# The entry of a streaming encoder trunk: memory keys and values in one loop, smaller first tiles, another inverse root

## The chip, the cores and the metric

One Trainium2 chip; the program runs on one of its cores. The metric is the device time of one execution in microseconds (us). A core has five engines with instruction queues of their own, each worked off in order: TensorE (PE in the profile, its weight loads PEld), VectorE (DVE), ScalarE (ACT), GpSimd (POOL) and SyncE (SP). They meet only at semaphores. Copies between the main memory and the core's two on-chip memories are issued here by SP, POOL and, in a few places, ACT. TensorE reads from the larger on-chip memory and writes its sums to eight banks of the smaller one, the PSUM.

## What is computed

The reference is a two-layer encoder for 512 tokens of width 1024, in float32. Only its beginning matters here:

```
def reference(x, mem, norm_mix_g, norm_ffn_g, a_w_in, ..., mem_w_kv, ...):
    for l in range(DEPTH):
        h = rmsnorm(x, norm_mix_g[l])
        if l < N_A_LAYERS:
            proj = h @ a_w_in[a]
            ...
        mem_out = memory_attention(q_mem, mem, mem_w_kv[l])
...
def memory_attention(q, mem, w_kv):
    mk, mv = jnp.split(mem @ w_kv, 2, axis=-1)
```

`mem` is 256 by 1024, `mem_w_kv` two matrices of 1024 by 512 (256 columns of keys, 256 of values). Since `mem @ mem_w_kv[l]` needs nothing of `x`, the kernel does it for both layers at its very start, while `x` is still being loaded. `rmsnorm` divides each row of `x` by the root of its mean square, so it needs one inverse root for each of the 512 tokens.

## The kernel before, in words

**Three products for one.** Every float32 matrix product is done as three products of shorter numbers. `split` (lines 139 to 144) makes of a tile its rounded high part, by a copy on ACT (line 140), and the rest, its low part, by a subtraction on DVE (line 141). `mm3` (lines 192 to 196) then issues high by high, high by low and low by high, one after the other, into the same PSUM bank. So a tile from memory can be used a first time when ACT has made its high part, a second time when DVE has made a low part, and so on.

**The entry** is lines 355 to 375 (loads) and 447 to 517. The loads are issued by SP in the order of the program: for q from 0 to 3 a tile `memr[q]` of the memory rows (256 KB) and a tile `kraw[q]` of the first layer's key weights (256 KB), then four tiles `vraw` of its value weights (256 KB each), two tiles `kraw1` of the second layer's key weights (512 KB each), `x` in four tiles of 512 KB, two tiles `vraw1` of the second layer's value weights, and from there the weights of the first projection. The three buffers tagged `wr` hold the 512 KB tiles in turn.

From line 447 on, the order of PE, ACT and DVE is that of the program: nothing is moved within each of these engines. It is:

- six small products of ones (`warm`, line 453), then a loop over q (lines 457 to 474): four transposes of `memr[q]` into one bank (line 462), `split` of the transposed tile, `split` of `kraw[q]`, and then the twelve key products of tile q - 1. In the first turn three more products of ones stand in their place. So the products of one tile hide the splitting of the next.
- a loop over the four value tiles (lines 476 to 481): `split`, then twelve value products each; between them, DVE copies the finished keys out of their two banks (`keep`, line 395), and POOL writes them to memory.
- `split` of the two `kraw1` tiles into the weight buffers `wh`/`wl`, and 48 key products of the second layer.
- the squares of `x` by ACT and DVE (lines 408 and 410), their sum and the inverse root `rsqrt` (lines 238 to 247: a shifted integer as a first guess and three steps of Newton, eleven instructions of DVE with 4 columns each), two diagonal matrices of it (line 256), `split` of `vraw1[0]`.
- eight `x_tile`s: four transposes of `x` on PE (line 417), a copy of 512 columns out of the bank by ACT (line 419). The banks go round: even tiles use tag `sc` (3 banks), odd tiles tag `tr` (2 banks), and a 106-column transpose of the small vectors takes a `tr` bank after tile 0. So tile 7 gets the bank that tile 3 had.
- `spread` (line 269): two products that lay the inverse roots along the columns; then the 48 value products of the second layer, from `vws1`, and beside them DVE and ACT scale and split the transposed `x` (lines 427, 432 and 435) for the first projection, `value_columns(1)`, whose first product with `x` is the first instruction of line 194 with 392 columns.

**Everything behind line 517** is ordered by a scheduler, which puts instructions of the later parts where it expects them to be ready. It starts from where the entry leaves the engines, so a change of the entry can move instructions far behind it.

## Time and profile before

| | |
|---|---|
| time, median of 3 runs | 1179.44 us (1178.71 to 1181.65) |
| the profiled execution | 1178.89 us, of which 1177.2 us from the first to the last instruction |
| PE busy | 1167.7 us (99% of the span), 7007 instructions |
| DVE busy | 941.1 us (80%), 1685 instructions |
| ACT busy | 730.3 us (62%), 1295 instructions |
| granted TensorE clock, mean | 0.999 |
| the chain that ended last | PE 95%, DVE 3%, ACT 1% |

The profile lists instructions with the time from the span's start, their duration, engine and line, what they write and read, and in brackets how long the engine had stood idle before and what ended that. Matmuls are pipelined: one of 256 columns lasts 0.28 us, but the next starts 0.12 us later, so the distance between starts says how fast PE goes.

### The profile page before, as it was taken

To read this page: it belongs to the slowest core of one execution; us is meant where nothing else is said; L and a number is where in the kernel's file an instruction comes from. 1 tells how busy PE (TensorE), PEld (TensorE's weight loads), DVE (VectorE), ACT (ScalarE), POOL (GpSimd) and SP (SyncE) were. 2 spreads that over 40 slices of the span, in tenths; PEclk is the share of its full clock that TensorE was granted. 3 is DMA by queue.
4 is the path that set the end of the run, shared out by engine and by line. 5 is a ranking of instruction groups with operands and counts; after the bars stand their busy time and mean duration, and the time that the engine had idled before them with its cause. 6 is when DMAs were issued, how large, how long until landed. Compare 5 with 4: busy or idle time off the path is not lost.

```text
span 1177.2 us, 18659 instructions
## 1 busy us (share of the span) xinstructions
PE 1167.7 (99%) x7007; PEld 1033.4 (88%) x7007; DVE 941.1 (80%) x1685; ACT 730.3 (62%) x1295; POOL 129.6 (11%) x222
## 2 busy tenths in 40 slices
PE   9999999999999999999999999999999999999997
PEld 9988888888889999999888888888889999999986
DVE  6877688887979887777698888897897887777755
ACT  6548677654656656665666667776565665666545
POOL 1111101000021111111020000101001011110100
PEclk9999999999999999999999999999999999999999
DMA  8645325243267766665564312335426456566551
GB/s 301 206 108 136 94 55 152 76 140 120 90 157 153 190 165 162 163 144 128 149 200 126 90 54 85 105 100 179 142 90 153 108 140 140 143 144 144 126 161 72
DMA packets 200445, 158.64 MB, mean 135 GB/s; under 512 B 8377, under 2 KB 180383, under 8 KB 200355
## 3 DMA queue, kind: packets, MB, share of 16 engines
q1 hardware_dynamic: 184194, 119.87, 34.5%
q0 software_dynamic: 15584, 36.67, 15.8%
q8 instruction: 55, 0.90, 0.3%
q10 hardware_dynamic: 576, 0.92, 0.2%
q14 instruction: 36, 0.29, 0.1%
HBM read 128.89 MB, written 32.46 MB: 137 GB/s over the span
## 4 chain that ended last, share of the span: by engine, by line
PE 95%; DVE 3%; ACT 1%; issue 0%; POOL 0%; POOLq 0%; DVEq 0%; ACTq 0%
PE pmm L194 18%; PE pmm L195 18%; PE pmm L196 18%; PE ptr L195 6%; PE ptr L194 6%; PE ptr L196 6%; PE psc L196 5%; PE psc L195 5%; PE psc L194 5%; PE psc L544 2%; PE ptr L1365 1%; PE ptr L1386 1%; PE ptr L1387 1%; PE ptr L627 1%; PE ptr L613 0%; DVE pt L141 0%
## 5 line engine op out<-in xcount | busy, mean ns | idle before, releaser
L194 PE MATMUL pmm<-u,wh 128*128 128x512 f32 (+1 forms) x968 | 333.0, 344 | 0.2 <-ACT u L140 0.2
L196 PE MATMUL pmm<-u,wl 128*128 128x512 f32 (+1 forms) x968 | 330.8, 342 | 0.0
L195 PE MATMUL pmm<-u,wh 128*128 128x512 f32 (+1 forms) x968 | 330.5, 342 | 0.0
L141 DVE TENSOR_TENSOR wl<-wr,wh 128x1024 fp32r<-128x1024 f32 (+3 forms) x172 | 199.8, 1163 | 82.0 <-ACT wh L140 81.5
L140 ACT CAST wh<-wr 128x1024 fp32r<-128x1024 f32 (+3 forms) x172 | 171.9, 1001 | 93.1 <-PE pmm L195 39.6
L196 PEld LDWEIGHTS pmm<-u,wl 128*128 128x128 f32 x968 | 181.9, 188 | 20.8
L194 PEld LDWEIGHTS pmm<-u,wh 128*128 128x128 f32 x968 | 181.8, 188 | 18.7 <-ACT u L140 1.1
L195 PEld LDWEIGHTS pmm<-u,wh 128*128 128x128 f32 x968 | 182.0, 188 | 18.4 <-DVE u L141 0.5
L194 PE MATMUL ptr<-u,wh 128*128 128x512 f32 x272 | 106.4, 391 | 0.0
L195 PE MATMUL ptr<-u,wh 128*128 128x512 f32 x272 | 106.2, 390 | 0.0
L196 PE MATMUL ptr<-u,wl 128*128 128x512 f32 x272 | 105.8, 389 | 0.0
L778 POOL DMA_DIRECT2D xspill<-t x64 | 55.5, 867 | 432.1 <-ACT t L777 419.6
L834 ACT COPY t<-pmm 128x256 f32<-128x256 f32 x102 | 38.2, 374 | 76.7 <-PE pmm L196 76.5
L141 DVE TENSOR_TENSOR u<-t,u 128x512 fp32r<-128x512 f32 (+1 forms) x94 | 54.2, 600 | 35.4 <-ACT u L140 35.4
L194 PE MATMUL pmm<-u,fh 128*128 128x256 f32 x272 | 75.4, 277 | 0.0
L195 PE MATMUL pmm<-u,fh 128*128 128x256 f32 x272 | 75.2, 277 | 0.0
L196 PE MATMUL pmm<-u,fl 128*128 128x256 f32 x272 | 75.1, 276 | 0.0
L196 PE MATMUL psc<-u,wl 128*128 128x256 f32 (+1 forms) x232 | 75.1, 324 | 0.0
L195 PE MATMUL psc<-u,wh 128*128 128x256 f32 (+1 forms) x232 | 75.1, 324 | 0.0
L194 PE MATMUL psc<-u,wh 128*128 128x256 f32 (+1 forms) x232 | 74.9, 324 | 0.0
L141 DVE TENSOR_TENSOR fl<-pt,fh 128x512 fp32r<-128x512 f32 x102 | 70.4, 690 | 5.1 <-ACT fh L140 1.4
L140 ACT CAST fh<-pt 128x512 fp32r<-128x512 f32 x102 | 62.8, 616 | 9.2 <-DVE pt L888 6.0
(334 smaller groups left out, 2509.1 us busy)
## 6 DMA issues: line engine op xcount, KB each, us to landing
wr<-in_ffn_w_up_dram SPq DMA_DIRECT2D x54, 512.0 KB, 6.0
wr<-in_ffn_w_down_dram SPq DMA_DIRECT2D x38, 512.0 KB, 5.5
pt<-in_ffn_w_up_dram SPq DMA_DIRECT2D x34, 512.0 KB, 7.7
xspill<-t POOLq DMA_DIRECT2D x64, 256.0 KB, 4.3
wr<-in_a_w_in_dram SPq DMA_DIRECT2D x20, 512.0 KB, 3.8
wr<-in_w_kv_dram SPq DMA_DIRECT2D x12, 512.0 KB, 4.1
xspill<-fh POOLq DMA_DIRECT2D x16, 256.0 KB, 2.6
xspill<-fl POOLq DMA_DIRECT2D x16, 256.0 KB, 3.1
```

The source lines that it names most:

```text
L140: high = A.copy(hi, src) if on_act else V.tensor_copy(hi, src)
L141: low = V.tensor_tensor(out=lo, in0=src, in1=f(hi), op=ALU.subtract)
L194: nc.tensor.matmul(o, lh, rh, start=first, stop=False, skip_group_check=more)
L195: nc.tensor.matmul(o, lh, rl, start=False, stop=False, skip_group_check=more)
L196: nc.tensor.matmul(o, ll, rh, start=False, stop=last, skip_group_check=more)
L544: nc.tensor.matmul(o, a, b, start=first and i == 0, stop=i == 1)
L627: nc.tensor.matmul(o2, vs[a][:, 2 * hp + h, :], p[h][:, a, :], start=i == 0, stop=i == 3)
L778: G.dma_start(xspill[j], t, accum_op=ALU.add)
L834: A.copy(o, r[:, :H])
L1365: nc.tensor.transpose(tp[:, b * P : (b + 1) * P], es[T, h][:, b * P : (b + 1) * P], ident)
L1386: nc.tensor.matmul(o2[:, s * P :], w, hi_at(pts[h], s, s, TT - s), start=s == 0, stop=False)
L1387: nc.tensor.matmul(o2[:, s * P :], w, lo_at(pts[h], s, s, TT - s), start=False, stop=s == TT - 1)
```

## The change

It is made in the entry alone; all the rest of the program text is as it was.

- **Loads.** The first memory tile and the first key tile come in two halves of 128 KB (one row tile of 128 rows each); one of the four halves is issued by ACT instead of SP. Each value tile is issued right after the key tile of the same q, where before all value tiles came after all key tiles.
- **First step.** Five products of ones instead of six at the start, one instead of three later. The two row tiles of tile 0 are transposed into two banks, and split in pieces of 256 columns. DVE makes the first high part of the keys. The first six products are ordered by part.
- **One loop.** For q from 1 to 3: transposes of tile q, `split` of the transposed tile, of the key tile and of the value tile; then the value products of tile q - 1 and the key products of tile q itself. After the loop: `keep` of the keys, and the last twelve value products.
- **Second keys.** The two `kraw1` tiles are split into the same two weight buffers as before, with the 16 columns of spare room at the end of the high part and at the start of the low part, and not the other way round.
- **Inverse root.** ACT takes the logarithm and the exponential with factor -0.5 (two instructions of 4 columns), DVE makes one Newton step (three instructions). The table of ACT that holds both functions is loaded once, at the start.
- **`vraw1[0]`** is split after the third `x_tile` and no longer ahead of the first, and the second layer's value products are issued in the order of their parts: all high by high, then all low by high, then all high by low.

```diff
         def scale(self, o):
-            v = small()
+            v, r, t, self.col = small(), small(), small(), small()
             V.tensor_scalar(v, o, 1.0 / D, EPS, op0=ALU.mult, op1=ALU.add)
-            self.col = small()
-            rsqrt(self.col, v)
+            A.activation(t, o, AF.Ln, scale=1.0 / D, bias=eps)
+            A.activation(r, t, AF.Exp, scale=-0.5)
+            V.tensor_mul(t, r, r)
+            V.scalar_tensor_tensor(t, t, -0.5, v, op0=ALU.mult, op1=ALU.mult)
+            V.scalar_tensor_tensor(self.col, t, 1.5, r, op0=ALU.add, op1=ALU.mult)
...
+    for i, queue in enumerate((nc.scalar, nc.sync)):
+        load_memory(0, i * P, P)
+        queue.dma_start(kraw[0][:, i : i + 1, :], rows(mem_w_kv[0], 0, MEM, i, i + 1))
+    nc.sync.dma_start(vraw[0], rows(mem_w_kv[0], MEM, MEM, 0, 2))
+    for q in range(1, KT // 2):
+        load_memory(q, 0, MEM)
+        nc.sync.dma_start(kraw[q], rows(mem_w_kv[0], 0, MEM, 2 * q, 2 * q + 2))
+        nc.sync.dma_start(vraw[q], rows(mem_w_kv[0], MEM, MEM, 2 * q, 2 * q + 2))
...
+    def value_products_by_parts(os_, wh, wl, k0):
+
+        n = wh.shape[1]
+        for part, w in ((0, wh), (1, wh), (0, wl)):
+            for k in range(n):
+                for m, o in enumerate(os_):
+                    a = memT[k0 + k][part][:, m * P : (m + 1) * P]
+                    first = k0 + k == 0 and part == 0 and w is wh
+                    nc.tensor.matmul(o, a, w[:, k, :], start=first, stop=w is wl and k0 + k == KT - 1)
...
+        logarithms()
...
-        warm(6)
...
+        warm(5)
...
+        (kh, kl), (hi, lo) = kws[0], parts_of[0]
+        for i, tag in enumerate(("tr", "sc")):
+            c = slice(i * MEM, (i + 1) * MEM)
+            tp = memory_rows(0, tag, (i,))
+            A.copy(hi[:, c], tp[:, c])
+            if i:
+                A.copy(kh[:, i, :], kraw[0][:, i, :])
+                V.tensor_tensor(out=lo[:, c], in0=tp[:, c], in1=f(hi)[:, c], op=ALU.subtract)
+            else:
+                V.tensor_copy(kh[:, i, :], kraw[0][:, i, :])
+            V.tensor_tensor(out=kl[:, i, :], in0=kraw[0][:, i, :], in1=f(kh)[:, i, :], op=ALU.subtract)
+            if not i:
+                V.tensor_tensor(out=lo[:, c], in0=tp[:, c], in1=f(hi)[:, c], op=ALU.subtract)
+        split(*vws[0], vraw[0])
+        warm(1)
...
+        for q in range(1, KT // 2):
+            tp = memory_rows(q, ("sc", "tr")[q % 2], range(2))
+            split(*parts_of[q], tp)
+            split(*kws[q], kraw[q])
+            split(*vws[q], vraw[q])
+            value_products(vo, *vws[q - 1], 2 * (q - 1))
+            key_products(ko, *kws[q], 2 * q)
+        keep(0, 0, ko)
+        value_products(vo, *vws[KT // 2 - 1], KT - 2)
+        kws1 = [parts(w, block=u) for u, w in enumerate(kraw1)]
...
-        vws1 = [parts(vraw1[0])]
         x_tile(0)
         load_vectors(0, 1, A.copy)
         for j in range(1, KT):
             x_tile(j)
+            if j == 2:
+                vws1 = [parts(vraw1[0])]
...
-        value_products(vo, *vws1[0], 0)
+        value_products_by_parts(vo, *vws1[0], 0)
...
-        value_products(vo, *vws1[1], 4)
+        value_products_by_parts(vo, *vws1[1], 4)
```

How the order of the engines changes is shown at three places. The numbers behind the names are those of the tiles; in the rows of PE the bank comes first, then the two operands.

First the loop. On PE before, the transposes of the third tile (`u_117`) are followed by the key products of the second (`u_184` to `u_189`, into the banks `pmm_161` and `pmm_162`):

```order
17 L462 MATMUL ptr_204<-ident,u_117 128x128 x4
18 L194 MATMUL pmm_161<-u_184,u_188 128x256
19 L195 MATMUL pmm_161<-u_185,u_188 128x256
20 L196 MATMUL pmm_161<-u_184,u_189 128x256
21 L194 MATMUL pmm_162<-u_184,u_188 128x256
22 L195 MATMUL pmm_162<-u_185,u_188 128x256
23 L196 MATMUL pmm_162<-u_184,u_189 128x256
24 L194 MATMUL pmm_161<-u_184,u_188 128x256
```

After the change, on PE, the transposes of the second tile (`u_110`) are followed by the value products of the first (`u_173` and `u_174` are the parts of its value weights, `pmm_206` and `psc_207` the banks), and then by the key products of the second tile itself, whose parts `u_183` and `u_184` are made from those very transposes, `u_167` and `u_168` from its key tile:

```order
26 L196 MATMUL pmm_206<-u_173,u_182 128x256
27 L194 MATMUL psc_207<-u_173,u_181 128x256
28 L195 MATMUL psc_207<-u_174,u_181 128x256
29 L196 MATMUL psc_207<-u_173,u_182 128x256
30 L194 MATMUL pmm_163<-u_183,u_167 128x256
31 L195 MATMUL pmm_163<-u_184,u_167 128x256
32 L196 MATMUL pmm_163<-u_183,u_168 128x256
33 L194 MATMUL pmm_164<-u_183,u_167 128x256
```

What moved: the key products stood one turn behind their transposes, and now stand in the same turn, with twelve value products between.

Second the `x` tiles on ACT. Before, the cast of the second value weights (`wh_438`, 1024 columns) stands ahead of the eight copies (`fh`, `fl`):

```order
20 L408 ACTIVATE t_410,s_150<-pt_126 128x512
21 L140 CAST wh_438<-wr_146 128x1024
22 L419 COPY fh_447<-psc_442 128x512
23 L345 COPY cols_451<-ptr_449 128x106
24 L419 COPY fh_458<-ptr_453 128x512
25 L419 COPY fh_465<-psc_460 128x512
26 L419 COPY fh_472<-ptr_467 128x512
27 L419 COPY fl_479<-psc_474 128x512
```

After, ACT takes the logarithm and the exponential, and the cast (`wh_463`) stands between the third and the fourth copy:

```order
22 L427 ACTIVATE t_415,s_152<-pt_136 128x512
23 L313 ACTIVATE s_422<-s_152,eps 128x4
24 L314 ACTIVATE s_421<-s_422 128x4
25 L438 COPY fh_443<-psc_438 128x512
26 L348 COPY cols_447<-ptr_445 128x106
27 L438 COPY fh_454<-ptr_449 128x512
28 L438 COPY fh_461<-psc_456 128x512
29 L140 CAST wh_463<-wr_148 128x1024
30 L438 COPY fh_472<-ptr_467 128x512
31 L438 COPY fl_479<-psc_474 128x512
```

What moved: 1024 columns of ACT's work went from ahead of the copies to between them.

Third, far behind the entry, one of the stretches that the scheduler ordered anew, in the second layer's attention on PE. Transposes of memory attention (`ptr_8187`, line 613 before and 660 after) and its products with the values (`ptr_8197`, line 627 or 674) stand among the products of a projection (`pmm_8227`). Before:

```order
4186 L194 MATMUL pmm_8227<-u_6466,wh_8223 128x512
4187 L195 MATMUL pmm_8227<-u_6467,wh_8223 128x512
4188 L196 MATMUL pmm_8227<-u_6466,wl_8224 128x512
4189 L194 MATMUL pmm_8227<-u_6504,wh_8223 128x512
4190 L195 MATMUL pmm_8227<-u_6505,wh_8223 128x512
4191 L196 MATMUL pmm_8227<-u_6504,wl_8224 128x512
4192 L613 MATMUL ptr_8187<-ident,t_8151 128x128 x4
4193 L544 MATMUL psc_8258<-u_7884,u_7990 128x128
4194 L627 MATMUL ptr_8197<-pt_8075,u_7979 128x512 x2
```

After:

```order
4187 L194 MATMUL pmm_8227<-u_6466,wh_8223 128x512
4188 L660 MATMUL ptr_8187<-ident,t_8151 128x128 x2
4189 L195 MATMUL pmm_8227<-u_6467,wh_8223 128x512
4190 L660 MATMUL ptr_8187<-ident,t_8151 128x128 x2
4191 L196 MATMUL pmm_8227<-u_6466,wl_8224 128x512
4192 L674 MATMUL ptr_8197<-pt_8075,u_7979 128x512 x2
4193 L674 MATMUL ptr_8197<-pt_8075,u_7982 128x512 x2
4194 L194 MATMUL pmm_8227<-u_6504,wh_8223 128x512
```

What moved: the transposes and the value products come up to five products of the projection earlier. Rows 4176 to 4420 of PE hold some twenty such moves; ACT and DVE are ordered anew beside them, and a few rows move right behind the entry, around PE's row 291. All other rows of the program stand as before.

More of the change, by code (lines that the diff above doesn't have):

```diff
@@ L475, in trunk, with memory_rows @@
-        vo = two_banks("mm", "sc")
-        for u in range(4):
-            vws.append([sb("u", [P, S], F32R).rearrange("p (a b) -> p a b", a=2) for _ in range(2)])
-            split(*vws[u], vraw[u])
-            if u == 0:
-                keep(0, 0, ko)
-            value_products(vo, *vws[u], 2 * u)
-        kws1 = [parts(w) for w in kraw1]
+        def memory_rows(q, tag, ks):
+            tp = ps(tag)
+            for i in ks:
+                for m in range(2):
+                    nc.tensor.transpose(
+                        tp[:, (2 * i + m) * P : (2 * i + m + 1) * P], memr[q][:, m, i * P : (i + 1) * P], ident
+                    )
+            return tp
@@ new lines, in high_low, with halved @@
+        def high_low():
+            return [sb("u", [P, S], F32R) for _ in range(2)]
+        def halved(pair):
+            return [t.rearrange("p (a b) -> p a b", a=2) for t in pair]
+        warm(5)
+        ko = two_banks("mm", "mm")
+        kws = [halved(high_low()) for _ in range(KT // 2)]
+        vws = [halved(high_low()) for _ in range(KT // 2)]
+        parts_of = [high_low() for _ in range(KT // 2)]
+        for hi, lo in parts_of:
+            for i in range(2):
+                memT.append((hi[:, i * MEM : (i + 1) * MEM], lo[:, i * MEM : (i + 1) * MEM]))
```

39 lines of the change are left out of this document (10 added, 29 removed).

## The prediction

> **What bounds the kernel now.** I read the page first, then, since the change is in the entry, the order of time on PE, ACT and DVE up to the first product with `x`.
>
> ```profile
> span 1177.2 us, 18659 instructions
> PE 1167.7 (99%) x7007; PEld 1033.4 (88%) x7007; DVE 941.1 (80%) x1685; ACT 730.3 (62%) x1295; POOL 129.6 (11%) x222
> ...
> GB/s 301 206 108 136 94 55 152 76 140 120 90 157 153 190 165 162 163 144 128 149 200 126 90 54 85 105 100 179 142 90 153 108 140 140 143 144 144 126 161 72
> ...
> PE 95%; DVE 3%; ACT 1%; issue 0%; POOL 0%; POOLq 0%; DVEq 0%; ACTq 0%
> ```
>
> PE works for 1167.7 of 1177.2 us and is 95% of the chain that ended last. A gain must come from the 9.5 us in which PE stands still or from products that follow each other slowly; a loss comes from every wait that PE is given. PE in the entry (start, duration, then in brackets idle time and what ended it):
>
> ```profile
> 1.13 2.93 PE L453 MATMUL pmm<-ones 128*128 128x128 f32 x12 [1.13 <-DVE mcf L127]
> 3.85 0.95 PE L462 MATMUL ptr<-ident,u 128*128 128x128 f32 x4
> 4.64 0.83 PE L453 MATMUL pmm<-ones 128*128 128x128 f32 x6
> ...
> 8.11 0.60 PE L462 MATMUL ptr<-ident,u 128*128 128x128 f32 x4
> 8.46 0.36 PE L194 MATMUL pmm<-u,u 128*128 128x256 f32 x1
> 8.66 0.28 PE L195 MATMUL pmm<-u,u 128*128 128x256 f32 x1
> ...
> 12.12 0.28 PE L195 MATMUL pmm<-u,u 128*128 128x256 f32 x1
> 12.58 0.39 PE L196 MATMUL pmm<-u,u 128*128 128x256 f32 x1 [0.17 <-DVE u L141]
> ...
> 13.88 0.28 PE L194 MATMUL pmm<-u,u 128*128 128x256 f32 x1
> ...
> 19.64 0.28 PE L194 MATMUL pmm<-u,wh 128*128 128x256 f32 x1
> ...
> 25.40 0.60 PE L417 MATMUL psc<-ident,pt 128*128 128x128 f32 x4
> ...
> 28.63 0.60 PE L417 MATMUL ptr<-ident,pt 128*128 128x128 f32 x4
> 28.98 0.71 PE L269 MATMUL psc<-t,onesr 128*128 128x512 f32 x2
> 29.53 0.28 PE L194 MATMUL pmm<-wh,u 128*128 128x256 f32 x1
> ...
> 35.32 0.34 PE L194 MATMUL pmm<-wh,u 128*128 128x392 f32 x1
> ```
>
> The second layer's 48 key products take 19.64 to 25.40, 0.12 us each: PE at its pace. The wait of 0.17 us at 12.58 shows where it is not: a product needs a low part that DVE has just finished. From 25.40 on PE does not wait. So the question is when, after the change, the `x` tiles begin (25.40 now), the value products (29.53 now) and the first product with `x` (35.32 now); what is late there is late at the end.
>
> **The loop.** ACT and DVE beside the transposes at 8.11, and DVE at the end of the keys and for the second keys:
>
> ```profile
> 8.74 0.59 ACT L140 CAST u<-ptr 128x512 fp32r<-128x512 f32 x1 [1.45 <-PE ptr L462]
> ```
> ```profile
> 9.36 0.69 DVE L141 TENSOR_TENSOR u<-ptr,u 128x512 fp32r<-128x512 f32 x1 [1.26 <-ACT u L140]
> 9.97 0.68 DVE L141 TENSOR_TENSOR u<-u,u 128x512 fp32r<-128x512 f32 x1
> ...
> 13.72 0.79 DVE L395 COPY u<-pmm 128x256 f32<-128x256 f32 x2 [0.59 <-PE pmm L196]
> ...
> 16.22 2.35 DVE L141 TENSOR_TENSOR wl<-wr,wh 128x1024 fp32r<-128x1024 f32 x2
> ```
> ```profile
> 2.32 0.47 SPq L359 DMA_DIRECT2D u<-in_mem_w_kv_dram  x1
> ```
> ```profile
> u<-in_mem_w_kv_dram SPq DMA_DIRECT2D x1, 256.0 KB, 4.2
> ```
>
> Start. Ten passes of ones instead of twelve, at 0.227 us (12 from 1.13 to 3.85), end at 3.4. Two transposes at 0.2 us, an ACT copy of half the width: the first product comes near 4.6 instead of 6.0, the first twelve end near 6.2. What a transfer of 128 KB takes, no row shows; it matters only if it holds up the second tile.
>
> Second tile. It now stands behind 768 KB, so its end is that of the first MB. Before, the load that ended the first MB was issued at 2.32 and landed 4.2 us later, at 6.5. I take 6.5 for its transposes; not before 6.2, when PE is free; and not after 7.4, which is 256 KB more at the page's 301 GB/s.
>
> A turn. From 8.11 to 8.66 are four transposes and one product, so the transposes cost 0.43. Twelve value products take 1.44: the key products are due 1.87 us after the transposes, their third, which needs the low part of the keys, at 2.11. That part comes from DVE's second subtraction, 9.97 + 0.68 - 8.11 = 2.54 us after the transposes, 2.60 with the 0.06 that PE needed to see it at 12.58 (11.84 + 0.68). **A wait of 0.49 us in each of three turns**, and 0.43 + 1.44 + 1.44 + 0.49 = 3.80 us a turn. It is the wait of 12.58, now in every turn: the splitting of a tile is covered by as many products as before. The value tile's third split is on ACT and DVE only (0.5 and 0.6 us more a turn) and ends before its products, a turn later. From 6.5: transposes at 10.3 and 14.1, keys done at 17.9, the last twelve value products at 19.35.
>
> Second keys. DVE's `keep` began 0.16 us ahead of the keys' end (13.72 against 13.88), so at 17.74; two copies of 0.35, then 1.18 us for the low part (2.35 for two): 19.6, seen at 19.7. PE wants it two products after 19.35, at 19.6: 0.1 us of waiting. DVE frees the two buffers at 20.8 instead of 18.57 (16.22 + 2.35), and `vraw1[1]` and the first projection's weights are issued behind that; ACT wants the first of them near 30.8, ten us later, so this costs nothing. All that is loaded ahead of `x` is the same 4 MB, so I let `x` land as before. The offsets in the weight buffers change no instruction's size; I price them at nothing, and at 0.05 us either way. 48 products: **the `x` tiles begin at 19.45 + 5.76 = 25.2**, with the bounds above 24.9 to 26.1. The gain of 1.4 us at the start is given back by the load and by three waits.
>
> **The x tiles.** ACT there, and DVE's inverse root:
>
> ```profile
> 23.11 0.63 ACT L408 ACTIVATE t<-pt 128x512 f32<-128x512 f32 x1 [0.62 <-DMA pt<-in_x_dram]
> ...
> 24.67 1.05 ACT L140 CAST wh<-wr 128x1024 fp32r<-128x1024 f32 x1 [0.84 <-DMA wr<-in_mem_w_kv_dram]
> 26.04 0.59 ACT L419 COPY fh<-psc 128x512 f32<-128x512 f32 x1 [0.32 <-PE psc L417]
> ...
> 27.13 0.62 ACT L419 COPY fh<-psc 128x512 f32<-128x512 f32 x1
> 27.61 0.63 ACT L419 COPY fh<-ptr 128x512 f32<-128x512 f32 x1
> ...
> 30.00 1.14 ACT L502 CAST wh<-wr 128x1024 fp32r<-128x1024 f32 x1
> 30.95 0.47 ACT L395 COPY u<-pmm 128x256 f32<-128x256 f32 x1
> ...
> 54.66 0.21 ACT L1050 ACTIVATE gate<-gate 128x16 f32<-128x16 f32 x1 [0.70 <-DVE gate L1049]
> ```
> ```profile
> 24.43 0.17 DVE L241 TENSOR_SCALAR s<-s  128x4 int32<-128x4 int32 x1
> ...
> 26.42 0.16 DVE L247 SCALAR_TENSOR_TENSOR s<-s,s 128x4 f32<-128x4 f32 x1
> ...
> 26.90 1.28 DVE L256 TENSOR_TENSOR t<-ident,s 128x512 fp32r<-128x512 f32 x2
> ...
> 33.86 0.69 DVE L435 TENSOR_TENSOR u<-t,u 128x512 fp32r<-128x512 f32 x1
> ```
>
> Before, the cast at 24.67 fell into a hole of ACT: it waited 0.84 us for its load, and after it ACT still waited 0.32 us for PE. It was free. Now it stands behind the third copy, and costs ACT 0.95 us (30.00 to 30.95). From 25.2: the first copy at 25.84 (0.64 after the transposes, as 26.04 after 25.40), the third done with its slot at 25.84 + 1.57 = 27.41 (27.61 - 26.04), the cast until 28.36, tile 3's copy until 29.0. Tile 7 needs tile 3's bank: its transposes, at 25.2 + 3.23 = 28.43 by PE's own pace, wait until 29.0, **0.57 us**. `spread` follows 0.35 and the value products 0.90 us later: 29.9 instead of 29.53.
>
> The inverse root: eleven instructions at 0.2 us (24.43 to 26.42) become two of ACT, about 0.25 us each by the row at 54.66, and three of DVE, some 1.1 us less. The diagonals, done at 28.18, would be done near 27.1. But `spread` was at 28.98 behind PE's own transposes, so the gain is hidden, now and after. The products by parts want the low part of `vws1[0]` 16 products after 29.9, at 31.8; it is there near 29.7 (the cast at 28.36, then 1.2 us of DVE). In the old order it would be wanted 0.12 us after 29.9, also in time: nothing is gained here either.
>
> 48 value products: 35.32 - 29.53 = 5.79, so the first product with `x` comes at 35.7, **0.4 us later than now**. ACT is 0.76 us late by then (four copies after 28.36, the next cast at 30.76 instead of 30.00); the low part of the first `x` tile, begun at 33.86 and done at 34.55, can be that late and still be in time for 36.0. One table load of ACT, between the exponential at 54.66 and the logarithm behind it, falls away; PE works on there without a wait.
>
> So the span grows by 0.4 us, with the bounds of the entry by 0.1 to 1.3. On the profiled execution's 1178.89 us that is 1179.3. The median of the runs shown lies 0.55 us above that execution, so I forecast **1179.9 us**. What a measurement can tell from no change is about 0.3%, 3.5 us; the forecast is well within.
>
> **The clock at the start.** The passes of ones cost 0.227 us each up to 3.85, the six from 4.64 about 0.11: PE works at half its pace for the first 3.4 us or so. The change takes three of these products away and puts waits for loads in their place. The Trainium skill ("TensorE: Matmul & The Clock Gate", Part 1 and Part 4) says that the clock rises after about 3.4 us of sustained work, in a window that runs freely, and that transposes do not count as work in the same way. The rise between 3.85 and 4.64 agrees with the 3.4 us; what transposes count for, no row here shows. By that rule the twelve first products could still be slow: the second rival.
>
> **Rivals.**
>
> 1. *The entry is fed better* (the load or DVE is quicker than I took it). Its gain has a floor: ACT's copies stand behind logarithm and exponential, which wait for the sum of squares, whose last square is that of 23.11; DVE had it at 24.4. With 0.5 us for the two, the first copy is at 24.8 at the earliest, so tile 7 waits for tile 3's copy until 24.8 + 1.57 + 0.95 + 0.62 = 27.9, the value products come at 28.8: 0.7 us gained, 1178.7.
> 2. *The clock rises one window late.* Twelve products at 0.22 instead of 0.12 end at 7.4 instead of 6.2, so the second tile begins 0.9 us after the 6.5 of the forecast, and the next twelve, in part slow, lose up to 0.8 us less the wait of 0.49 that they cover: 0.9 to 1.2 us on top of the forecast, 1181.0. Still within what counts as no change.
> 3. *Slower: the second layer's attention.* Before, this is how a wait looks there:
>
> ```profile
> 752.86 0.45 PE L194 MATMUL pmm<-u,wh 128*128 128x512 f32 x1
> 753.49 0.73 PE L627 MATMUL ptr<-pt,u 128*128 128x512 f32 x2 [0.18 <-DVE pt L141]
> ```
>
>  0.63 us from start to start, of which a product of 512 columns needs 0.23: 0.4 us lost, because the products with the values came before DVE had made their low part. The change moves such groups up at some twenty places. If ten of them meet their ACT or DVE as this one did, 4 us are lost, 1183.9. It decides from nine such waits on. Against it: moves go both ways, and the wait of 753.49 may itself vanish.
> 4. *Faster by the same reordering*: it would have to take away nine such waits, and the rows above show that one of 0.4 us is already listed with 0.18 only; few are listed at all. 1175.9.
>
> **How the numbers follow.** Forecast 0.58; better fed 0.14; clock 0.12; slower by the attention 0.11; faster by it 0.05. So faster 0.05, same 0.84, slower 0.11. The range must hold 0.8: it takes in the first rival with the spread of the runs below it (1177.8), and above the clock rival, the late load (1180.7) and a part of the attention's waits (seven of 0.4, 1182.6).
>
> **What would show it.** Right: transposes of tiles 2 and 3 about 3.8 us apart, each turn's third key product with a wait on DVE of 0.2 to 0.5 us; `x` tiles at 24.9 to 26.1; a gap on PE ahead of the last `x` tile that ends with tile 3's copy; the first product with 392 columns at 35.3 to 36.6. Wrong: `x` tiles at 24 or before; no gap ahead of tile 7; products that start 0.2 us apart after 5 us; waits of some us between 735 and 815.

## The result and the profile after

The changed kernel takes **1181.71 us** (median of 19 runs, 1180.59 to 1182.06), the kernel before 1179.26 (19 runs, 1178.71 to 1181.77): a ratio of 1.0017 with a 95% interval of 1.0009 to 1.0024. That is slower by 2.45 us: less than the 0.3% that the prediction took for the least that can be told, but the interval lies above 1, so the loss is small and real. 1179.9 was forecast, with a range of 1177.8 to 1182.6. Between the two profiled executions the span grew by 2.2 us, from 1177.2 to 1179.4; the profiled execution of the changed kernel (1181.06) is the second fastest of its 19 and lies 0.65 us below their median. From the page of the changed kernel:

```profile
span 1179.4 us, 18645 instructions
...
PE 1168.4 (99%) x7001; PEld 1032.0 (88%) x7001; DVE 941.4 (80%) x1680; ACT 729.0 (62%) x1297; POOL 129.3 (11%) x222
```

PE is busy 0.7 us longer and stands still 1.5 us longer (11.0 instead of 9.5). The order of time on PE in the entry shows where the larger part of the loss, 1.5 of the 2.2 us, arises (start, duration, in brackets idle time and what ended it):

```profile
3.81 0.66 PE L479 MATMUL ptr<-ident,u 128*128 128x128 f32 x2 [0.18 <-DMA u<-in_mem_dram]
...
4.93 0.97 PE L517 MATMUL pmm<-u,u 128*128 128x256 f32 x6
6.18 0.39 PE L194 MATMUL pmm<-u,u 128*128 128x256 f32 x1 [0.27 <-ACT u L505]
...
7.10 0.28 PE L196 MATMUL pmm<-u,u 128*128 128x256 f32 x1
7.31 0.66 PE L479 MATMUL ptr<-ident,u 128*128 128x128 f32 x4
...
9.97 0.39 PE L196 MATMUL pmm<-u,u 128*128 128x256 f32 x1 [0.17 <-DVE u L141]
...
11.27 0.60 PE L479 MATMUL psc<-ident,u 128*128 128x128 f32 x4
...
15.17 0.60 PE L479 MATMUL ptr<-ident,u 128*128 128x128 f32 x4
...
26.21 0.60 PE L436 MATMUL psc<-ident,pt 128*128 128x128 f32 x4
...
29.01 0.60 PE L436 MATMUL psc<-ident,pt 128*128 128x128 f32 x4
30.05 0.66 PE L436 MATMUL ptr<-ident,pt 128*128 128x128 f32 x4 [0.44 <-ACT fh L438]
30.46 0.72 PE L269 MATMUL psc<-t,onesr 128*128 128x512 f32 x2
...
36.76 0.34 PE L194 MATMUL pmm<-wh,u 128*128 128x392 f32 x1
```

The first product comes at 4.93 instead of 6.00, as the change means it to. But the second tile's transposes stand at 7.31, the turns take 3.96 and 3.90 us with a wait for DVE in each (it is shown for the first), the `x` tiles begin at 26.21 (25.40 before), and PE waits ahead of the last of them for ACT's copy. The first product with `x` comes 1.44 us later than before (36.76 against 35.32). What ACT did there:

```profile
27.95 0.62 ACT L438 COPY fh<-psc 128x512 f32<-128x512 f32 x1
28.43 1.08 ACT L140 CAST wh<-wr 128x1024 fp32r<-128x1024 f32 x1
29.38 0.62 ACT L438 COPY fh<-ptr 128x512 f32<-128x512 f32 x1
```

The cast of 1.08 us stands ahead of tile 3's copy, and tile 7 waits for the bank that this copy empties.

To see where the rest is lost, I set PE's sixteen products with the matrix of ones (`onesr`: those of `spread`, and from 279 us on those that sum a later norm) of the two traces side by side. The lag, by which the changed kernel is later than the one before, is 1.48 us at 29 us, 1.46 at 617 us, and **2.30 at 833 us**. So 0.84 us are lost between 617 and 833, in the second layer's attention. PE's waits of 700 to 830 us (releaser, us in total, times, longest), after the change:

```profile
PE psc L591 <- DVE s L1397: 0.3, 1, 0.3
PE ptr L660 <- DVE t L651: 0.3, 1, 0.3
PE psc L591 <- ACT t L648: 0.2, 1, 0.2
```

And before (line 544 there is line 591 after the change, and 613 is 660):

```profile
PE ptr L627 <- DVE pt L141: 0.2, 1, 0.2
PE psc L544 <- ACT t L601: 0.2, 1, 0.2
```

The order of this attention was written anew by the change, as the prediction said. Two new waits for DVE stand there, at 748 and 759 us; the one at 753.49 that the prediction shows is gone. The table counts idle time only; from one start to the next a wait costs PE more than that, so its numbers do not add up to the 0.84 us.

### The profile page after: what moved, and what is told of

Same layout as the page of the kernel before. It is cut to its first block, busy times and chain, and to the rows that moved or that the text cites. A ratio compares the mean times of both kernels' runs of the same rounds, so it can differ in the third digit from the quotient of the medians.

```text
span 1179.4 us, 18645 instructions
## 1 busy us (share of the span) xinstructions
PE 1168.4 (99%) x7001; PEld 1032.0 (88%) x7001; DVE 941.4 (80%) x1680; ACT 729.0 (62%) x1297; POOL 129.3 (11%) x222
## 3 DMA queue, kind: packets, MB, share of 16 engines
q10 hardware_dynamic: 720, 1.05, 0.2%
## 4 chain that ended last, share of the span: by engine, by line
PE 95%; DVE 2%; ACT 2%; issue 0%; DMA 0%; SPq 0%; POOL 0%; POOLq 0%; DVEq 0%; ACTq 0%
PE pmm L194 18%; PE pmm L196 18%; PE pmm L195 18%; PE ptr L195 6%; PE ptr L196 6%; PE ptr L194 6%; PE psc L196 5%; PE psc L195 5%; PE psc L194 5%; PE psc L591 2%; PE ptr L1412 1%; PE ptr L1433 1%; PE ptr L1434 1%; PE ptr L660 1%; PE ptr L674 0%
```

## The experiments

The theory, after the two traces: three terms make the loss. The second tile lands later and the turns wait for DVE (0.8 us at the `x` tiles); the cast between the copies (0.6); and the attention's order (0.85), which comes from one detail: the new inverse root takes four buffers of the 26 shared small ones where the old one took three in all, so every later scratch buffer is another one, and the order of work that follows from the buffers differs. Rivals for each: the order comes from something else in the change; the wait of the last tile comes from the late entry and not from the cast; the loss is in the clock. All runs, with the second tile's transposes, the start of the `x` tiles, and PE's lag behind the trace of before at three `spread` products (us; the ratio to before with its 95% interval):

| kernel | median | ratio | second tile | `x` tiles | lag 29 | lag 617 | lag 833 |
|---|---|---|---|---|---|---|---|
| the change | 1181.71 | 1.0009 to 1.0024 | 7.31 | 26.21 | 1.48 | 1.46 | 2.30 |
| before, one more buffer | 1179.79 | 1.0000 to 1.0017 | | 25.49 | 0.09 | 0.07 | 0.98 |
| three buffers | 1180.62 | 1.0004 to 1.0021 | 7.82 | 26.67 | 1.93 | 1.83 | 1.85 |
| cast ahead | 1181.59 | 1.0013 to 1.0032 | 6.82 | 25.66 | 0.27 | 1.28 | 2.19 |
| keys behind | 1180.13 | 1.0000 to 1.0018 | 7.13 | 25.20 | 0.46 | 0.58 | 1.52 |
| whole loads | 1182.49 | 1.0016 to 1.0033 | 7.94 | 26.84 | 2.10 | 3.01 | 3.95 |
| old inverse root | 1180.85 | 1.0003 to 1.0021 | 7.35 | 26.24 | 1.50 | 1.56 | 1.61 |
| before, cast between | 1179.96 | 0.9997 to 1.0014 | | 26.16 | 1.42 | 1.42 | 1.40 |
| three repairs | 1179.71 | 0.9994 to 1.0012 | 7.47 | 25.14 | 0.31 | 1.04 | 1.05 |
| keys behind, three buffers | 1179.48 | 0.9992 to 1.0010 | 8.14 | 25.84 | 1.11 | 1.09 | 1.07 |
| halves, second tile first | 1182.15 | 1.0014 to 1.0034 | 7.30 | 27.18 | 2.44 | 2.59 | 3.48 |
| whole, second tile first | 1182.46 | 1.0016 to 1.0036 | 7.61 | 26.70 | 1.95 | 3.01 | 3.87 |
| late cast | 1180.41 | 1.0000 to 1.0018 | 7.11 | 25.60 | 0.21 | 2.00 | 2.01 |

The kernel before had medians of 1179.02 to 1179.11 beside these runs. All the medians lie within 0.3% of it; where an interval takes in 1.0000, the time alone does not tell the kernel from the one before. The lags are those of one profiled execution each. The loads at the start land now earlier, now later, and the half pace at which PE starts ("The clock", further below) ends now earlier, now later: with the loads of the change unaltered, the second tile's transposes came at 6.82 to 8.14. So the columns on the left carry that much chance, and the difference between two lags of one trace does not.

### One more scratch buffer in the kernel before

```diff
-            v = small()
+            v, _ = small(), small()
```

> The kernel before with one more small buffer taken in the inverse root, never written; no instruction is added or removed, and the entry is that of before. Theory (the rotation of the shared small buffers alone makes the scheduler order the second layer's attention anew, and that order costs what the change lost there): first product with x at 35.3 as before, some 0.8 us more between 617 and 833 us, span about 1178.1. Rival (the attention is late because the changed entry hands its engines over otherwise): span 1177.2 as before.

The lag is 0.07 us at 617 and 0.98 at 833 us, with nothing changed but a buffer that nobody writes. The waits are those of the change:

```profile
PE psc L544 <- DVE s L1350: 0.3, 1, 0.3
PE ptr L613 <- DVE t L604: 0.3, 1, 0.3
PE psc L544 <- ACT t L601: 0.2, 1, 0.2
```

### Three scratch buffers in the change

```diff
-            v, r, t, self.col = small(), small(), small(), small()
+            v, r, t = small(), small(), small()
...
-            V.scalar_tensor_tensor(self.col, t, 1.5, r, op0=ALU.add, op1=ALU.mult)
+            self.col = v
+            V.scalar_tensor_tensor(v, t, 1.5, r, op0=ALU.add, op1=ALU.mult)
```

> The changed kernel, whose new inverse root takes three small buffers as the old one did (its last step writes in place). Theory: attention ordered and timed as before, first product with x late as in the change (36.8), span about 1178.6, 0.8 us under the change. Rival (the new entry itself delays the attention): span 1179.4 as the change.

1.83 us at 617 and 1.85 at 833: the loss in the attention is gone, and so are its two waits:

```profile
PE ptr L675 <- DVE pt L141: 0.2, 1, 0.2
PE psc L592 <- ACT t L649: 0.2, 1, 0.2
```

Over all thirteen kernels of the table the lag grows between 617 and 833 us by 0.84 to 0.94 in the seven with the extra buffer, and by -0.02 to 0.05 in the six without. The medians go the same way: 0.7 us more with the buffer in the kernel before (1179.79 against 1179.06 beside it), 1.1 less without it in the change. **This term is settled.**

### The cast ahead of the x tiles again

```diff
+        vws1 = [parts(vraw1[0])]
         x_tile(0)
...
-            if j == 2:
-                vws1 = [parts(vraw1[0])]
```

> The changed kernel with the cast of the second value weights ahead of the x tiles again. Theory (the cast is free there and costs 0.6 us between the copies): no wait ahead of the last x tile, x tiles at 26.2 as in the change, first product with x 9.9 us later at 36.1, span 0.6 us under the change. Rival (ACT's eight copies are the bound in any place): first product with x at 36.7 as in the change.

The wait for tile 3's copy is gone, and the lag at 29 us is 0.27 (1.48 with the change; 0.55 of the difference is the earlier start of the `x` tiles, 0.60 the wait). But at 133 us it is 1.25 and the median is that of the change. The trace shows the place: PE's only long stop between, where the last scores of the first scan are wanted:

```profile
28.89 0.60 PE L436 MATMUL ptr<-ident,pt 128*128 128x128 f32 x4
29.25 0.71 PE L269 MATMUL psc<-t,onesr 128*128 128x512 f32 x2
```
```profile
120.27 0.39 PE L196 MATMUL pmm<-u,wl 128*128 128x512 f32 x1
121.17 0.33 PE L194 MATMUL ptr<-pt,u 128*128 128x128 f32 x1 [0.52 <-ACT pt L140]
```

From 120.27 to 121.17 are 0.90 us where a product needs 0.23, and 0.33 instead of 0.06 follow: 0.9 to 1.0 us. I had expected neither. Ten us earlier SP and POOL ask for a weight tile and for exponents (issues on the two queues); first this run, then the run with keys behind:

```profile
109.76 0.37 SPq L153 DMA_DIRECT2D wr<-in_a_w_in_dram  x1
```
```profile
109.59 0.57 POOL L1090 DMA_DIRECT2D bias<-exponents  x1 [2.42 <-ACT t L1216]
```
```profile
109.68 0.37 SPq L153 DMA_DIRECT2D wr<-in_a_w_in_dram  x1
```
```profile
109.88 0.57 POOL L1093 DMA_DIRECT2D bias<-exponents  x1 [2.31 <-ACT t L1219]
```

With the weights 0.20 us ahead, ACT could cast them 4.76 us after the issue; with the exponents 0.16 us ahead, 5.43 us after it. ACT's cast, the scan's exponential behind it, and PE follow late. Over all fourteen traces there are two cases and nothing between: nine with the weights 0.20 to 0.21 us ahead (4.1 to 4.8 us to the cast, no stop at 121 us), five with the exponents 0.16 to 0.17 ahead (5.2 to 5.4 us, and 0.8 to 1.0 us lost at 121). In those five DVE, whose work sets the weights' buffer free, began one instruction of the scan 0.36 us later (it stood 0.80 us where it stands 0.44), with PE's product for it no later. What holds DVE in these five kernels I could not find; they are the changed kernels with the cast moved or the first loads whole. That the later issue is the cause rests on these fourteen traces; no run put the order of the two issues right by itself.

### Key products one turn behind

```diff
+            if q > 1:
+                key_products(ko, *kws[q - 1], 2 * (q - 1))
             value_products(vo, *vws[q - 1], 2 * (q - 1))
-            key_products(ko, *kws[q], 2 * q)
+        key_products(ko, *kws[KT // 2 - 1], KT - 2)
         keep(0, 0, ko)
```

> The changed kernel with the key products one turn behind their transposes again, beside the value products of the same tile; every product is still made. Theory (three waits for the low part of the keys, 0.45 each, are made by the order; behind them the loads bound the loop): no wait of the third key product in any turn, but the third tile's transposes wait for its load near 10.5; x tiles at 25.6 to 25.9, 0.3 to 0.6 us earlier than the change. Rival 1 (the loads do not bound): x tiles at 24.9. Rival 2 (the loads alone set the loop): x tiles at 26.2 as in the change.

From the second tile's transposes to the `x` tiles it is 18.07 us (25.20 - 7.13) instead of 18.90 (26.21 - 7.31): 0.83 saved. The waits for DVE are gone, and a load has taken the place of the first:

```profile
9.94 0.66 PE L479 MATMUL psc<-ident,u 128*128 128x128 f32 x4 [0.79 <-DMA u<-in_mem_dram]
...
25.20 0.60 PE L436 MATMUL psc<-ident,pt 128*128 128x128 f32 x4
...
29.04 0.66 PE L436 MATMUL ptr<-ident,pt 128*128 128x128 f32 x4 [0.44 <-ACT fh L438]
```

Without DVE's wait it is the third memory tile's load that holds PE, as the theory had it, though at 9.94 and not near 10.5, and the `x` tiles come 0.4 us earlier than its 25.6. By the medians the step is worth more than the 0.83 of the trace: 1.6 us against the change, 1.1 between the two kernels with three buffers (1180.62 and 1179.48). Why the medians give more is open. The wait ahead of the last `x` tile is the same though the tiles begin a microsecond earlier.

### The first loads whole

```diff
-    for i, queue in enumerate((nc.scalar, nc.sync)):
-        load_memory(0, i * P, P)
-        queue.dma_start(kraw[0][:, i : i + 1, :], rows(mem_w_kv[0], 0, MEM, i, i + 1))
+    load_memory(0, 0, MEM)
+    nc.sync.dma_start(kraw[0], rows(mem_w_kv[0], 0, MEM, 0, 2))
```

> The changed kernel with the first tile and its key weights loaded whole, as before (two loads of 256 KB on SP instead of four of 128 KB on ACT and SP); the first step is still worked in row tiles. Theory (the small first loads cost transfer time): the second tile lands near 6.5 us instead of 6.7 to 7.4, its transposes come at about 6.9, the x tiles at 25.6 to 25.8 instead of 26.2, and the time is about 0.4 us below the change, 1181.3. Rival (the position behind 768 KB is what counts): the second tile lands at 7.0 to 7.3 all the same, the first product comes later because a whole 256 KB must land first (about 5.2 instead of 4.9), the x tiles stay at 26.2 or come later, and the time is that of the change or up to 0.3 us above it.

The theory fell: the second tile's transposes wait for its load until 7.94, later than with the halves and than the 7.3 of the rival, and the time is 0.8 us above the change, as much as this trace loses at 121 us in the second of the two cases above. Yet the halves do cost transfers. What moved in each microsecond (last column GB/s), before, after, and with whole loads:

```profile
3.00:4.00 1.00, 1.00 (x6) 1.00 (x6) 0.00 (x0) 0.00 (x0) 0.00 (x0) 1.00 1.03 334
4.00:5.00 1.00, 1.00 (x9) 1.00 (x8) 0.00 (x0) 0.16 (x1) 0.00 (x0) 1.00 0.86 283
```
```profile
3.00:4.00 1.00, 0.82 (x4) 0.55 (x4) 0.60 (x2) 0.00 (x0) 0.00 (x0) 1.00 0.91 192
4.00:5.00 1.00, 1.00 (x7) 0.97 (x6) 0.20 (x2) 0.44 (x2) 0.00 (x0) 1.00 0.62 140
```
```profile
3.00:4.00 1.00, 0.87 (x4) 0.61 (x4) 0.00 (x0) 0.00 (x0) 0.00 (x0) 1.00 1.08 346
4.00:5.00 1.00, 1.00 (x6) 0.92 (x5) 0.34 (x2) 0.48 (x2) 0.00 (x0) 1.00 0.69 218
5.00:6.00 1.00, 1.00 (x8) 0.82 (x7) 1.00 (x4) 1.00 (x3) 0.00 (x0) 1.00 0.76 239
```

Over the fourteen traces, the eight with halves had moved 0.59 to 0.72 MB by 5 us and 2.87 to 3.02 MB by 12 us, the six with whole loads 0.83 to 0.93 and 3.15 to 3.27. With whole loads the thin stretch comes as well, a microsecond later, while the second tile is due.

### The old inverse root in the change

```diff
-            v, r, t, self.col = small(), small(), small(), small()
+            v = small()
...
-            A.activation(t, o, AF.Ln, scale=1.0 / D, bias=eps)
...
+            self.col = small()
+            rsqrt(self.col, v)
```

> The changed kernel with the inverse root of before (eleven instructions of DVE, no logarithm and exponential; two scratch buffers, so that the second layer's attention stands in the order of before). Theory (the inverse root is hidden behind PE's transposes, and the extra scratch buffer is what costs 0.9 us late in the run): the gap ahead of the last x tile stays at about 0.4 to 0.6 us and ends with the copy of tile 3, spread stands at 30.4 to 30.9, and the time is that of the run with three scratch buffers, about 1180.6. Rival (the new inverse root does shorten the entry): spread comes up to 1.1 us later, near 31.5, and the time is about 1181.7.

With the one that `rsqrt` takes itself it uses three buffers, and it does what the run with three buffers does: 1180.85 against 1180.62, the same gap ahead of the last `x` tile, `spread` 4.24 us after the `x` tiles begin in both. The logarithm and exponential gain nothing, as forecast, since `spread` stands behind PE's transposes:

```profile
30.07 0.65 PE L433 MATMUL ptr<-ident,pt 128*128 128x128 f32 x4 [0.44 <-ACT fh L435]
```

### The cast between the copies, in the kernel before

```diff
-        vws1 = [parts(vraw1[0])]
         x_tile(0)
...
+            if j == 2:
+                vws1 = [parts(vraw1[0])]
```

> The kernel before with one line moved: ACT's cast of the first second-layer value weights stands behind the third x tile, as in the change. Theory: the x tiles begin at 25.4 as before, the last x tile's transposes wait 0.5 to 0.6 us for the copy of tile 3, the first product with 392 columns comes at about 35.9 instead of 35.32, and the span grows by 0.5 to 0.6, 1177.8; time about 1179.6. Rival (the wait belongs to the late entry, not to the place of the cast): no gap ahead of the last x tile, and the time of before, 1179.1.

The gap comes in the kernel before too, 0.60 us more from start to start than PE's pace:

```profile
28.95 0.60 PE L417 MATMUL psc<-ident,pt 128*128 128x128 f32 x4
30.00 0.66 PE L417 MATMUL ptr<-ident,pt 128*128 128x128 f32 x4 [0.44 <-ACT fh L419]
```

So it belongs to the place of the cast and not to a late entry alone: the `x` tiles begin at 26.16 here, but at 25.20 in the run with keys behind, and the wait is 0.60 in both. The rest of this trace's lag of 1.42, 0.8 us, is a slow start of this execution, whose loads are those of before: its first product with the memory stands at 6.86 instead of 6.00. The median is 0.94 above that of before beside it, more than the 0.60, and the interval takes in 1.0000; the difference stays open.

### Three repairs at once

The edits of three buffers, cast ahead and keys behind together.

> The changed kernel with three repairs at once: key products one turn behind their loads, the cast ahead of the x tiles, and three scratch buffers in the inverse root instead of four. If the three terms add up, the x tiles begin near 25.2, spread comes near 28.8, no wait is added in the second layer's attention, and the span is about 1177.0, the time about 1178.7, 0.4 us below the kernel before. Rival (gains of the entry are given back where the weights of the first scan are loaded, as in the run with the cast alone, when the exponents are asked for before the weights): spread near 28.8, but about 1 us lost between 110 and 122 us, span 1178, time about 1179.7.

The rival came true for the time: `x` tiles at 25.14, none added in the attention, and 1 us lost at 121 us, where the exponents were again asked for 0.16 us ahead of the weights. With the kernel before it is a draw. But the three terms did not add up in the entry either: `spread` stands at 29.29, not at 28.8. The cast, ahead of the copies again, had to wait for its own load until 25.40 and ended at 26.45, while PE began its `x` tiles 0.26 us earlier than before; so ACT's copies came late, and PE stood still ahead of the fourth tile (27.13, 0.57 us behind its pace):

```profile
PE ptr L437 <- ACT cols L349: 0.4, 1, 0.4
```

The cast is free ahead of the copies only if its load comes in time for that.

### Keys behind and three buffers

The same without the cast ahead.

> The changed kernel with key products one turn behind and three scratch buffers in the inverse root; the cast stays between the x tiles. Theory (the two terms add up, and the last weights of the first projection are again asked for ahead of the exponents): spread near 29.4, PE 0.5 us later than before at 133 us and at 833 us alike, span 1177.6, time about 1179.3. Rival (the loss near 120 us comes with any entry this early): PE 1.5 us later than before from 121 us on, time about 1180.2.

The weights were 0.20 us ahead, nothing was lost at 121 us, and 1179.48 is the best of the variants: a ratio of 1.0001 to before. The lag of its profile (1.07) is larger than the 0.5 forecast because its second tile landed late (transposes at 8.14, after 0.95 us of waiting for the load).

### The second tile's load ahead of the first value weights

```diff
-    nc.sync.dma_start(vraw[0], rows(mem_w_kv[0], MEM, MEM, 0, 2))
     for q in range(1, KT // 2):
         load_memory(q, 0, MEM)
+        if q == 1:
+            nc.sync.dma_start(vraw[0], rows(mem_w_kv[0], MEM, MEM, 0, 2))
```

With the halves of the change:

> The changed kernel with the load of the first value weights behind that of the second memory tile. Theory A (the hole in the transfers between 3 and 5 us belongs to the value weights standing third): the hole is gone or later, the second tile lands at 5.8 to 6.2, its transposes come behind the first twelve products at 6.6 to 6.9, the x tiles at 25.5 to 25.8, time 0.4 to 0.6 us below the change. Theory B (the hole belongs to the small first loads of 512 bytes a row, whatever follows): 140 to 200 GB/s between 3 and 5 us all the same, the second tile at 6.5, but PE waits for the second half of the first key weights until 6.2, x tiles at 26.0 to 26.2, time within 0.2 us of the change.

With whole first loads:

> Whole first loads (as in the run with whole loads), and the load of the first value weights behind that of the second memory tile, so that the first three loads are those of the kernel before. Theory A (the hole belongs to the value weights standing third): 280 GB/s or more from 2 to 6 us as before, the second tile lands at 5.5 to 6.0, x tiles at 25.7 to 26.0. Theory B (the hole comes when some number of loads is in flight, whatever they read): 220 to 240 GB/s between 4 and 6 us as with whole loads, the second tile at 6.5 to 7.2, the value weights at 7.9, x tiles at 26.5 or later.

With the halves the thin stretch stays (222 and 176 GB/s from 3 to 5 us) and the second tile lands at 7.26 as in the change, though 256 KB fewer stand ahead of it. That speaks for theory B and against A, but B's own numbers failed too: 6.5 for the tile, 26.2 for the `x` tiles (27.18), 0.2 us for the time (0.44 above the change). The entry also came late for a new reason: PE waited for the value weights that now stand behind it.

```profile
8.65 0.38 PE L194 MATMUL pmm<-u,u 128*128 128x256 f32 x1 [0.69 <-ACT u L140]
9.38 0.39 PE L195 MATMUL pmm<-u,u 128*128 128x256 f32 x1 [0.34 <-DVE u L141]
```

With whole loads 318, 263 and 308 GB/s move from 3 to 6 us, and the second tile lands at 6.35: neither theory's numbers quite, nearer to A. Nothing is gained, because PE did not reach its transposes before 7.61; its products stood 0.21 us apart until then.

### A late cast

Keys behind, three buffers, whole loads with the second tile first, and the cast behind the sixth `x` tile (`j == 5` instead of `j == 2`).

> The changed kernel with what the runs so far favour: key products one turn behind, three scratch buffers in the inverse root, whole first loads with the first value weights behind the second memory tile, and the cast of the second layer's first value weights behind the sixth x tile, where the tile that shares a bank with the last one has been copied already. Theory: the transfers reach 1.35 MB or more by 7 us (halves: 1.2 to 1.35), the x tiles begin at 24.8 to 25.2, there is no gap ahead of the last x tile, spread stands at 28.4 to 28.8, 0.2 to 0.6 us ahead of before, and PE keeps that lead to the end if the weight load near 110 us is asked for ahead of the exponents: time 1178.5. Rival (that load falls behind the exponents again, as in the runs with the cast moved ahead): 1 us is lost near 121 us and the time is about 1179.5.

No gap ahead of the last `x` tile and a lag of 0.21 at 29 us, but the value products waited for the cast itself, 0.7 us:

```profile
29.19 0.71 PE L269 MATMUL psc<-t,onesr 128*128 128x512 f32 x2
30.42 0.39 PE L410 MATMUL pmm<-wh,u 128*128 128x256 f32 x1 [0.51 <-ACT wh L140]
```

The wait had only moved by one step, and the exponents were again ahead of the weights (1 us at 121). No version of the twelve beats the kernel before.

## Why the prediction was right, and by which steps it was off

The range held, and the mechanism of the entry; the forecast itself was low. It had 0.4 us of growth worked out, and 2.2 came (span; 2.45 by the medians). Of that, 1.5 us arose in the entry, where the prediction looked, and 0.8 us in the attention, for which its sum had nothing. That the total fell into the range is in part luck: the upper end was stretched for seven waits in the attention, and two new ones came. Of the signs that it named, the distance of the transposes, the waits for DVE and the gap ahead of the last `x` tile came as written; the `x` tiles (26.21) and the first product with 392 columns (36.76) came just behind their bounds of 26.1 and 36.6.

- **Start: mis-sized.** First product at 4.93 (forecast 4.6), the first twelve done at 7.2 (forecast 6.2). The prediction had priced the halved loads at nothing unless they held up the second tile. They held up the first one: its transposes waited for the load until 3.81, and the second half of the key weights reached ACT only at 5.72, so that PE waited 0.27 us in the middle and lost 0.4 from start to start.

```profile
5.72 0.40 ACT L505 CAST u<-u 128x256 fp32r<-128x256 f32 x1 [0.42 <-DMA u<-in_mem_w_kv_dram]
```

- **Second tile: mis-sized as well.** The step "its end is that of the first MB", 6.5, took the rate of before for loads that were now cut into halves. The traces with halves had moved about a quarter less by 5 us. The tile landed at 7.26, its transposes came at 7.31, 0.81 us later than forecast and just inside the bound of 7.4. In this trace PE was done with the first twelve products at 7.22, so each of the two terms alone would have cost 0.7 us or more: with the tile in time PE would have come at 7.2 all the same. In four other traces with the same loads (transposes at 6.82, 7.13, 7.47 and 7.82) the tile had landed 0.1 to 0.4 us before PE was done, in one (8.14) PE waited 0.95 us for it. Whether the row length of 512 bytes, the second queue or the number of loads thins the stretch from 3 to 5 us, the runs do not tell apart.
- **Turns.** A wait of 0.49 us in each was forecast; from start to start they were 0.33, 0.46 and 0.46, and the turns 3.96 and 3.90 for 3.80 (PE's first products behind each wait and each group of transposes start 0.20 to 0.26 us apart). From the second tile's transposes to the `x` tiles 18.90 us were measured and 18.7 forecast. The run with keys behind shows that these waits were real and that a load stands right behind the first of them.
- **The cast.** 0.57 forecast, 0.60 measured, in the change and when put into the kernel before alone. This step was right as it stands: the bank, the copy and the size.
- **Inverse root, products by parts, block buffers.** Priced at nothing; the old root in the change confirms the first. The other two were not tried apart; from the `spread` products to the first product with `x` it takes 6.30 us after and 6.34 before.
- **The attention.** Priced at nothing in the forecast, with 0.11 for a loss of 4 us and 0.05 for a gain. It lost 0.84 us in the change: the direction and the kind of the third rival, waits for DVE, with two new ones and not nine. What the prediction had missed is where the new order came from: the number of scratch buffers taken by the inverse root, not the inverse root.
- **The clock.** The second rival did not happen in the profile of the change, where from the second to the sixth the products behind 4.93 start 0.12 us apart. It did in other traces with the same order on PE. In the run with whole loads and the second tile first:

```profile
4.97 1.63 PE L517 MATMUL pmm<-u,u 128*128 128x256 f32 x6
6.40 0.41 PE L194 MATMUL pmm<-u,u 128*128 128x256 f32 x1
...
7.25 0.40 PE L195 MATMUL pmm<-u,u 128*128 128x256 f32 x1
```

  There the products stand 0.21 us apart until 7.4, as the passes of ones do at the start of every trace. Over the fourteen traces this slow stretch ends between 4.5 and 7.7 us. Among them are three that load and begin as before: 4.6 in the kernel before, 6.4 with one more buffer, 6.8 with the cast between. So it varies without the change, and nothing here shows that the change makes it longer. That the window of the clock runs freely, as the Trainium skill says ("TensorE: Matmul & The Clock Gate", Part 1), agrees with this. The stretch is worth some 0.5 us at the second tile (7.82 in the run with three buffers, against 7.31). The profile of the change is one with a short stretch; whether longer ones make the 0.65 us by which the median lies above it, no run shows.

## What to carry to other kernels

A buffer taken from a rotation is part of the schedule: a single scratch buffer more, never written, brought 0.9 us of waiting 700 us later, so compare the order of the whole program and not only of the edited part. An early gain is worth what the next meeting of two queues leaves of it: in five of these traces 0.8 to 1.0 us were lost again, and in each of them two loads, 0.2 us apart, had changed places. And an operation that stands in a hole between two waits is free there only while the hole lasts: the cast cost nothing ahead of the copies in the kernel before, 0.6 between them, 0.7 behind them, and 0.6 ahead of them too where its load came later and the work behind it earlier.

## What had not been expected of the hardware

Cutting two loads of 256 KB into four of 128 KB (rows of 512 bytes for the memory tile) went with 115 to 229 GB/s in the microsecond from 4 to 5, where 218 to 301 came with whole loads; the two ranges touch (229 with the cast ahead, 218 with whole loads). The packets themselves explain little of it (median 27 ns for 512 bytes, 46 ns for 1024, in the trace of the change): in that microsecond the DMA engines were busy for 62% of the time, against 86% before, and single packets of 1024 bytes took up to 1.05 us between 3 and 5 us. The Trainium skill ("DMA: Bandwidth & Descriptors", Specifications) gives 512 bytes as the size from which a transfer runs at line rate; by that the rows of 512 bytes should have cost nothing. The packets show a little of that cost, 19 against 22 GB/s an engine, and the slow microseconds went with the halves; the measurement decides, though it does not separate the row's length from the smaller loads.

The granted clock reads 1.00 in all the rows by microsecond above (the third column from the end), also between 3 and 4 us, where PE's passes of ones (before) still start 0.21 us apart, twice the 0.11 of those from 4.64 on. For the first microseconds the pace of the products is the thing to read, and not that column.
